# Binding gathered expert rows to their place on two engines in a hybrid decoder layer

## The chip, the cores and the metric

The kernel runs on one core of a Trainium2 chip. Its time is the device time of one launch in microseconds (us), and lower is better. Five engines work side by side, each through a queue of its own that runs in order: TensorE (PE, with its weight loads as PEld), VectorE (DVE), ScalarE (ACT), GpSimd (POOL) and SyncE (SP). SP and POOL also issue DMA transfers. The order within a queue is fixed when the kernel is built.

## The reference, cut to what matters

One decoder layer on 512 tokens of width 1024: an mLSTM and a sliding-window attention share a projection, a cross-attention over 256 memory tokens follows, and then a retrieval from 16,384 experts of one neuron each. All that matters here is the retrieval:

```python
v1, i1 = lax.top_k(s1, 16)            # per token and head: best 16 of 128 first keys
v2, i2 = lax.top_k(s2, 16)            # and of 128 second keys
top_s, pos = lax.top_k(cand_s, 16)    # best 16 of the 256 sums -> expert i1 * 128 + i2
g = jax.nn.softmax(top_s, axis=-1)
u = expert_down[eidx]
a = jax.nn.gelu(jnp.einsum('thkd,td->thk', u, xb), approximate=False)
coef = g * a
return jnp.einsum('thk,thkd->td', coef, expert_up[eidx])
```

There are eight heads, so each token uses 128 experts.

## The kernel before, in words

The 512 tokens are four blocks of 128. The front of the layer, the cross-attention and the top-k run first. The retrieval is then done in two ways.

**Block 0: by rows.** `gather` (line 696) is a generator. Each of its 256 steps fetches one row per token, 128 rows of 4 KB, with an indirect DMA on POOL's queue (`fetch`, line 705), and uses it on DVE: the first 128 steps multiply a row of `expert_down` with the tokens and sum it to one number (`dots`, line 711), and the last 128 add a row of `expert_up`, times its coefficient, to the sum `gacc` (line 721; the first one is line 719). Eight buffers hold rows, so eight fetches can be ahead of DVE.

**Blocks 1 to 3: densely.** For each of the 128 values of the second key, called i2, a "down" tile computes all activations of 128 experts for 384 tokens, and an "up" tile multiplies them with the gates and with the 128 rows of `expert_up`. `Down` (line 755) splits the weights into a high part on ACT (`dh`) and a low part on DVE (`dl`, line 766), runs 24 matmuls, three for each of eight slices of the width (lines 777 to 779), and a Gelu. `up_tile` (line 798) splits its weights in the same way (`uh` on ACT, `ul` on DVE, line 822), multiplies activations by gates on DVE (`cf`, line 829), rounds on ACT (`ch`, line 831) and takes the rest on DVE (`cl`, line 832). `up_mm` (line 836) runs its 18 matmuls. 68 of the 128 down tiles are made early, between other work, and parked in DRAM; five more follow in a lead, and the other 55 are made between the up steps. `up_order` and `made_by(u)` say which tiles go when: `made_by(u)` is the number of down tiles that have been traced by up step u. A ring of ten buffers lets down tiles run ahead of their up steps.

**The gates.** The dense way needs a 128 x 128 table of gates for each token. For block 1, `scatter` (line 611) builds it in DRAM: 128 indirect DMAs on POOL's queue, 16 for each head, add one gate for each token (line 630), and the additions of one head wait for those of the head before. The last 16 are kept in `c.sc[HD - 1]`. For blocks 2 and 3, `gating` (line 639) builds it with one-hots: 32 steps of four tokens for each block, 64 in all. Each step makes a first one-hot for all four tokens (`onehot`, on ACT in even steps and on DVE in odd ones, line 661), four second one-hots times the gate on DVE (line 683, four buffers), and a matmul for each token (line 684). `early.fill(3)` puts nine matmuls of an early down tile behind each step's matmuls.

**What sets the order.** A planner orders each queue on a simulated timeline before the kernel runs. It takes what is ready, earlier code first. `tc.issue_after(x)` restricts it: every instruction that the block under it issues on the engine of x must stand behind x in that queue. It is an order, not a wait. In the kernel before, eight of the 256 row steps are called in the gating of block 3, one in every fourth step (`GEV = 4`), under `issue_after(mm)`. `mm` is a matmul on PE, and a row step issues nothing on PE, so this binds none of its instructions: the planner may put the fetch and the product wherever they seem to fit. The other 248 row steps are called in the first 122 up steps (`GST`), about two for each, behind `c.dl`, the low part of the latest down tile, on DVE. Their fetches on POOL are free.

Of the kernel before, what the change touches and what calls it, by code (L numbers as in the profile page):

```python
# [17 lines left out]
ALU = mybir.AluOpType  # L18
# [3 lines left out]
P = 128  # L22
# [3 lines left out]
NB = S // P  # L26
# [4 lines left out]
HD = 8  # L31
TK = 16
NK = 128
# [10 lines left out]
FGT0 = KT  # L44
# [3 lines left out]
assert SP == SG * UG and (sum(FRT) + FEND) % KT == 0  # L48


GEV = 4
GST = 122

LEAD = 5
# [11 lines left out]
def f32(ap):  # L66
    return ap.bitcast(F32)
# [571 lines left out]
def gating(c, early, ga):  # L639

    nc, ps, gs, mp = c.nc, c.ps, c.gs, c.mp
    V, A, T = nc.vector, nc.scalar, nc.tensor
    for b in range(NG + NS, NB):
        tr = []
        for n_, src in (("I1T", c.I1), ("I2T", c.I2), ("gT", c.gg)):
            tp = ps.tile([P, 512], F32, tag="a", name="tp_i")
            T.transpose(tp[:, :P], src[:, b].rearrange("p h k -> p (h k)"), c.ident)
            o = gs.tile([P, P], F32, tag=n_, bufs=1, name=n_)
            A.copy(o, tp[:, :P])
            tr.append(o)  # L650
        i1, i2, g = tr
        n1 = gs.tile([P, P], F32, tag="n1", bufs=1, name="n1")
        A.mul(n1, i1, -1.0)
        io = c.iota.unsqueeze(1).to_broadcast([P, 4, P])

        def onehot(q):

            o1 = gs.tile([P, 4, P], F32, tag="oh1", bufs=5, name="oh1")
            ib = i1[:, 4 * q:4 * q + 4].unsqueeze(2).to_broadcast([P, 4, P])
            if q % 2:  # L660
                V.tensor_tensor(o1, io, ib, op=ALU.is_equal)
            else:
                for t1 in range(4):
                    t = 4 * q + t1
                    A.activation(o1[:, t1], c.iota, AF.Abs, bias=n1[:, t:t + 1])
                A.activation(o1, o1, AF.Relu, bias=1.0, scale=-1.0)
            return o1

        oh = [onehot(q) for q in range(3)]
        if b == NG + NS:  # L670
            early.fill(FGT0)
        for q in range(32):
            if q % 8 == 0:
                stg = gs.tile([P, NK, 32], F32, tag="stg", bufs=2, name="stg")
            if q + 3 < 32:
                oh.append(onehot(q + 3))
            o1 = oh[q]
            w = ps.tile([P, 512], F32, tag="b", name="w")
            w4 = w.rearrange("p (i t) -> p i t", t=4)
            for t1 in range(4):  # L680
                t = 4 * q + t1
                o2 = gs.tile([P, P], F32, tag="oh2", bufs=4, name="oh2")
                V.tensor_scalar(o2, c.iota, i2[:, t:t + 1], g[:, t:t + 1], op0=ALU.is_equal, op1=ALU.mult)
                mm = T.matmul(w4[:, :, t1], o1[:, t1], o2, start=True, stop=True)
            q8 = q % 8
            A.copy(stg[:, :, 4 * q8:4 * q8 + 4], w4)
            if q8 == 7:
                nc.sync.dma_start(c.wd[b - NG][:, :, 32 * UG * (q // 8):32 * UG * (q // 8 + 1)].rearrange("g p i -> p g i"),
                                  stg.rearrange("p (g i) t -> p g (i t)", i=UG))
            with c.tc.issue_after(mm.ins):  # L690
                early.fill(FGT)
                if b == NB - 1 and q % GEV == GEV - 1:
                    step(ga, 1)


# [29 lines left out]
def split3(c, pool, raw, tag, bufs):  # L725
    hi = pool.tile([P, D], F32R, tag=tag + "h", bufs=bufs, name=tag + "h")
    lo = pool.tile([P, D], F32R, tag=tag + "l", bufs=bufs, name=tag + "l")
    c.nc.scalar.copy(hi, raw)  # L728
    return hi, lo
# [68 lines left out]
def up_tile(c, u, i2, gel, acc):  # L798
    nc, up = c.nc, c.up
    V, A, T = nc.vector, nc.scalar, nc.tensor  # L800
    if i2 % UG == 0:
        c.wt = up.tile([P, ND, UG * P], F32, tag="wt", bufs=2, name="wt")
        for b in range(ND):
            i = nc.sync.dma_start(c.wt[:, b], c.wd[b][i2 // UG])
            for j in c.sc[HD - 1] if b == 0 else ():
                c.tc.add_manual_dep(i.ins, j.ins.name, SYNC, reason="gates complete")
        if i2 < SP:
            c.gsr = c.gl.tile([P, UG, TD], F32, tag="gsr", bufs=2, name="gsr")
            nc.sync.dma_start(c.gsr, c.gd[i2 // UG])
    if i2 % GRP == 0:  # L810
        c.uraw = up.tile([P, GRP, D], F32, tag="uraw", bufs=2, name="uraw")
        nc.sync.dma_start(c.uraw, c.a["up"].rearrange("(i p) d -> p i d", p=P)[:, i2:i2 + GRP])
    g = c.gsr[:, i2 % UG] if i2 < SP else gel[i2]
    raw = c.uraw[:, i2 % GRP]
    last = u == NK - 1
    if last:
        z = c.xlo.rearrange("p k t -> p (k t)")
        hi, lo = z[:, 0:D], z[:, D:2 * D]
        A.copy(hi, raw)
    else:  # L820
        hi, lo = split3(c, up, raw, "u", 2)
    V.tensor_tensor(lo, raw, f32(hi), op=ALU.subtract)  # L822
    cf = up.tile([P, TD], F32, tag="cf", bufs=2, name="cf")
    if last:
        ch, cl = z[:, 2 * D:2 * D + TD], z[:, 3 * D:3 * D + TD]
    else:
        ch = up.tile([P, TD], F32R, tag="ch", bufs=2, name="ch")
        cl = up.tile([P, TD], F32R, tag="cl", bufs=2, name="cl")
    V.tensor_tensor(cf.rearrange("p (b t) -> p b t", t=32), g.rearrange("p (b t) -> p b t", t=32),  # L829
                    c.wt.rearrange("p b (q i t) -> p (b q) i t", q=4, i=UG)[:, :, i2 % UG], op=ALU.mult)  # L830
    A.copy(ch, cf)  # L831
    V.tensor_tensor(cl, cf, f32(ch), op=ALU.subtract)  # L832
    return hi, lo, ch, cl


# [200 lines left out]
def body(tc, a, out, dbg=None):  # L1036
    c = Ctx()
    c.tc, c.nc, c.a = tc, tc.nc, a
    nc = c.nc
    with ExitStack() as st:  # L1040
# [47 lines left out]
        def ahead(n):  # L1088
            for _ in range(n):
                gel.append(Down(c, len(gel)).mm().out())  # L1090

        with ExitStack() as tk:
            c.tk = tk.enter_context(pool("topk"))
            early = Early(c, gel)
# [3 lines left out]
        with pool("gather", side="right") as c.gp:  # L1098
            ga = gather(c)
# [1 line left out]
                gating(c, early, ga)  # L1101
            c.up = st.enter_context(pool("up"))
            assert len(gel) == SP
            ahead(LEAD)
            pst_ = [c.ps.tile([P, 512], F32, tag=t, name="acc_u") for t in "bbbbaa"]
            acc = [[pst_[2 * b], pst_[2 * b + 1]] for b in range(ND)]
            last = []
            g0 = 32 // GEV
            for u, i2 in enumerate(up_order()):
                ahead(made_by(u) - len(gel))  # L1110
                with tc.issue_after(c.dl.ins):
                    step(ga, (2 * P - g0) * (u + 1) // GST - (2 * P - g0) * u // GST)
                parts = up_tile(c, u, i2, gel, acc)
                if u >= NK - 2:
                    last.append(parts)
                else:
                    for b in range(ND):
                        up_mm(c, u, parts, acc, b)
# [15 lines left out]
def made_by(u):  # L1134

    return min(NK, SP + LEAD + (u + 1) * (NK - SP) // NK)
# [16 lines left out]
def step(it, n):  # L1153
    for _ in range(n):
        next(it, None)
# [49 lines left out]
```

## Time and profile before

| | |
|---|---|
| median of 3 runs | 1722.9 us (1717.44 to 1725.04) |
| the profiled execution | 1724.66 us, of which its span 1723.0 us |
| busy: PE, PEld | 1640.4 us (95%), 1428.0 us (83%) |
| busy: DVE, ACT, POOL | 1236.0 us (72%), 724.5 us (42%), 602.9 us (35%) |
| moved by DMA | 400.58 MB, 232 GB/s over the span |
| mean granted TensorE clock | 0.98 |

The span is the time from the first to the last instruction of one execution. Busy shares are means over stages. The front, cross-attention and top-k take up to about 707 us, the gating runs from 713 to 912 us, the lead to 935 us and the up steps to 1704 us. A row of the timeline or of the groups names line, engine, operation, and what it writes and reads; in brackets or behind the bar stands how long the engine was idle before it and what ended that.

### The profile page before, as it was taken

What the parts mean: (1) busy time and instruction counts of PE and PEld (TensorE: products, weight loads), DVE (VectorE), ACT (ScalarE), POOL (GpSimd) and SP (SyncE); (2) the same over time, 40 slices, a digit from 0 to 9 for tenths busy, and PEclk for the clock granted to TensorE, in tenths of its full rate; (3) what the DMA queues carried; (4) which work ended last, traced back from release to release, by engine and by line L of the source; (5) the groups of instructions that cost most, each with busy time, mean ns of one, the idle gap of its engine ahead of it and who ended that gap; (6) DMA issues with size and microseconds to landing.
All of it is one profiled execution on the core that took longest, in us unless ns stands there. A gap on an engine that the chain in (4) does not pass through costs nothing. (4 is left out here: it accounts for less than half of the span.)

```text
span 1723.0 us, 22949 instructions
## 1 busy us (share of the span) xinstructions
PE 1640.4 (95%) x8366; PEld 1428.0 (83%) x8368; DVE 1236.0 (72%) x2701; ACT 724.5 (42%) x1206; POOL 602.9 (35%) x427
## 2 busy tenths in 40 slices
PE   7999999999999999559999999999999999999897
PEld 5776588878999999559998888988888888888676
DVE  5535565464778888557775988878888888888965
ACT  5434544343544544437873333333333333332333
POOL 2000000000027878887003544444444443444400
PEclk9997999999999999879999999999999999999999
DMA  6135035232254435648778999988999998988952
GB/s 208 72 145 220 25 122 174 96 137 111 92 180 120 111 93 135 184 120 264 251 227 299 409 359 350 341 324 341 338 364 375 349 350 336 348 327 315 402 198 86
DMA packets 149105, 400.58 MB, mean 232 GB/s; under 512 B 28144, under 2 KB 62080, under 8 KB 136320
## 3 DMA queue, kind: packets, MB, share of 16 engines
q1 hardware_dynamic: 89232, 255.76, 40.8%
q0 software_dynamic: 55360, 134.32, 23.1%
q10 hardware_dynamic: 4400, 9.04, 1.4%
q8 instruction: 65, 1.06, 0.2%
q14 instruction: 48, 0.39, 0.1%
HBM read 356.28 MB, written 42.80 MB: 232 GB/s over the span
## 5 line engine op out<-in xcount | busy, mean ns | idle before, releaser
L777 PE MATMUL acc_d<-xhi,dh 128*128 128x384 f32 x1024 | 351.2, 343 | 3.6 <-ACT gel L788 3.6
L779 PE MATMUL acc_d<-xhi,dl 128*128 128x384 f32 x1024 | 345.2, 337 | 1.7 <-DVE dl L766 1.7
L778 PE MATMUL acc_d<-xlo,dh 128*128 128x384 f32 x1024 | 344.3, 336 | 0.0
L844 PE MATMUL acc_u<-ul,ch 128*128 128x512 f32 x762 | 295.8, 390 | 5.9 <-DVE ul L822 5.9
L845 PE MATMUL acc_u<-uh,cl 128*128 128x512 f32 x762 | 294.6, 390 | 0.0
L705 POOL DMA_INDIRECT rows<-in_down_r_dram,eidx x128 | 177.7, 1388 | 296.5 <-DVE dots L711 276.4
L630 POOL DMA_INDIRECT wd<-gg,ei x128 | 230.4, 1800 | 138.1 <-DVE ei L624 87.3
L705 POOL DMA_INDIRECT rows<-in_up_dram,eidx x128 | 170.5, 1332 | 189.7 <-DVE gacc L721 167.9
L831 ACT CAST ch<-cf 128x384 fp32r<-128x384 f32 x127 | 65.1, 514 | 382.9 <-PE acc_u L844 230.0
L843 PE MATMUL acc_u<-uh,ch 128*128 128x512 f32 x762 | 216.0, 392 | 9.9 <-ACT uh L728 8.7
L766 DVE TENSOR_TENSOR dl<-draw,dh 128x1024 fp32r<-128x1024 f32 x128 | 156.2, 1222 | 72.5 <-ACT dh L728 60.4
L777 PEld LDWEIGHTS acc_d<-xhi,dh 128*128 128x128 f32 x1024 | 194.0, 189 | 8.9 <-ACT gel L788 4.7
L779 PEld LDWEIGHTS acc_d<-xhi,dl 128*128 128x128 f32 x1024 | 193.3, 189 | 4.7 <-DVE dl L766 2.6
L778 PEld LDWEIGHTS acc_d<-xlo,dh 128*128 128x128 f32 x1024 | 193.8, 189 | 2.6
L728 ACT CAST dh<-draw 128x1024 fp32r<-128x1024 f32 x128 | 134.1, 1049 | 140.6 <-PE acc_d L778 116.1
L711 DVE CUSTOM_DVE_ANT_0 rows<-rows,xn 128x1024 f32<-128x1024 f32 x128 | 153.4, 1219 | 35.1 <-DMA rows<-in_down_r_dram,eidx 35.0
L843 PEld LDWEIGHTS acc_u<-uh,ch 128*128 128x128 f32 x762 | 141.9, 188 | 39.5 <-ACT uh L728 11.2
L844 PEld LDWEIGHTS acc_u<-ul,ch 128*128 128x128 f32 x762 | 142.9, 188 | 37.0 <-DVE ul L822 7.8
L845 PEld LDWEIGHTS acc_u<-uh,cl 128*128 128x128 f32 x762 | 143.1, 188 | 29.1
L721 DVE SCALAR_TENSOR_TENSOR gacc<-rows,coef,gacc 128x1024 f32<-128x1024 f32 x127 | 162.5, 1280 | 0.9
L822 DVE TENSOR_TENSOR ul<-uraw,uh 128x1024 fp32r<-128x1024 f32 x127 | 154.2, 1220 | 7.8 <-ACT uh L728 7.1
L832 DVE TENSOR_TENSOR cl<-cf,ch 128x384 fp32r<-128x384 f32 x127 | 70.8, 558 | 111.3 <-ACT ch L831 107.9
(333 smaller groups left out, 2672.0 us busy)
## 6 DMA issues: line engine op xcount, KB each, us to landing
draw<-in_down_t_dram SPq DMA_DIRECT2D x64, 1024.0 KB
uraw<-in_up_dram SPq DMA_DIRECT2D x64, 1024.0 KB
wt<-wd SPq DMA_DIRECT2D x96, 256.0 KB
wd<-stg SPq DMA_DIRECT2D x8, 2048.0 KB
gd<-gsp SPq DMA_DIRECT2D x17, 768.0 KB
gsr<-gd SPq DMA_DIRECT2D x17, 768.0 KB
wd<-zero ACTq DMA_DIRECT2D x1, 8192.0 KB
raw<-in_w_pq_dram SPq DMA_DIRECT2D x8, 1024.0 KB
```

Source lines behind the costliest of these rows:

```text
L630: i = G.indirect_dma_start(out=out, out_offset=bass.IndirectOffsetOnAxis(ap=ei[:, h, k:k + 1], axis=0), in_=c.gg[:, NG, hh, k:k + 1], in_o ...
L705: G.indirect_dma_start(out=r, out_offset=None, in_=src, in_offset=bass.IndirectOffsetOnAxis(ap=c.eidx[:, j:j + 1], axis=0))
L711: V.tensor_tensor_reduce(r, r, c.xn0, 1.0, 0.0, op0=ALU.mult, op1=ALU.add, accum_out=dots[:, j:j + 1])
L721: V.scalar_tensor_tensor(c.gacc, r, coef[:, j:j + 1], c.gacc, op0=ALU.mult, op1=ALU.add)
L766: c.dl = nc.vector.tensor_tensor(self.lo, raw, f32(self.hi), op=ALU.subtract)
L777: T.matmul(acc[:, :TD], self.hi[:, ks], c.xhi[:, k, NG * P:], start=(k == 0), stop=False)
L778: T.matmul(acc[:, :TD], self.hi[:, ks], c.xlo[:, k, NG * P:], start=False, stop=False)
L779: T.matmul(acc[:, :TD], self.lo[:, ks], c.xhi[:, k, NG * P:], start=False, stop=(k == KT - 1))
L822: V.tensor_tensor(lo, raw, f32(hi), op=ALU.subtract)
L843: T.matmul(acc[b][n], ch[:, t], hi[:, d], start=st, stop=False)
L844: T.matmul(acc[b][n], ch[:, t], lo[:, d], start=False, stop=False)
L845: T.matmul(acc[b][n], cl[:, t], hi[:, d], start=False, stop=sp)
```

## The change

It touches three places, and the counts that go with them.

1. In the gating of block 3, a row step is called in every second step from 9 to 31, twelve in all. Its fetch must stand behind the last addition of `scatter` on POOL, and its product behind the step's last one-hot on DVE. Nothing else moves a row step into the gating.
2. In the lead, eight row steps are spread over the five down tiles, each behind that tile's `c.dl` on DVE.
3. In the up steps, the first row step of step u is bound behind `c.cf`, the product with the gates, and any other behind `c.cl`. The 236 row steps left are spread by `due`, which counts one for each up step and one for each down tile made, up to step 121.

Besides, the 24 matmuls of `early.fill(FGT0)` are bound behind the third transpose of block 2's routes on PE.

```diff
-GEV = 4
+GQ = range(9, 32, 2)
+GLD = 8
 GST = 122
...
-            T.transpose(tp[:, :P], src[:, b].rearrange("p h k -> p (h k)"), c.ident)
+            tr_ = T.transpose(tp[:, :P], src[:, b].rearrange("p h k -> p (h k)"), c.ident)
...
         if b == NG + NS:
-            early.fill(FGT0)
+            with c.tc.issue_after(tr_.ins):
+                early.fill(FGT0)
...
-                V.tensor_scalar(o2, c.iota, i2[:, t:t + 1], g[:, t:t + 1], op0=ALU.is_equal, op1=ALU.mult)
+                last = V.tensor_scalar(o2, c.iota, i2[:, t:t + 1], g[:, t:t + 1], op0=ALU.is_equal, op1=ALU.mult)
...
             with c.tc.issue_after(mm.ins):
                 early.fill(FGT)
-                if b == NB - 1 and q % GEV == GEV - 1:
+            if b == NB - 1 and q in GQ:
+                with c.tc.issue_after(c.sc[HD - 1][-1].ins), c.tc.issue_after(last.ins):
                     step(ga, 1)
...
-    V.tensor_tensor(cf.rearrange("p (b t) -> p b t", t=32), g.rearrange("p (b t) -> p b t", t=32),
+    c.cf = V.tensor_tensor(cf.rearrange("p (b t) -> p b t", t=32), g.rearrange("p (b t) -> p b t", t=32),
...
-    V.tensor_tensor(cl, cf, f32(ch), op=ALU.subtract)
+    c.cl = V.tensor_tensor(cl, cf, f32(ch), op=ALU.subtract)
...
-            ahead(LEAD)
+            for n in range(LEAD):
+                ahead(1)
+                with tc.issue_after(c.dl.ins):
+                    step(ga, GLD * (n + 1) // LEAD - GLD * n // LEAD)
...
-            g0 = 32 // GEV
+            g0 = len(GQ) + GLD
+
+            due = [u + made_by(u) for u in range(-1, GST)]
+            rows = [(2 * P - g0) * (d - due[0]) // (due[-1] - due[0]) for d in due]
+            rows += [rows[-1]] * (NK - GST)
             for u, i2 in enumerate(up_order()):
                 ahead(made_by(u) - len(gel))
-                with tc.issue_after(c.dl.ins):
-                    step(ga, (2 * P - g0) * (u + 1) // GST - (2 * P - g0) * u // GST)
                 parts = up_tile(c, u, i2, gel, acc)
+                for i in range(rows[u + 1] - rows[u]):
+                    with tc.issue_after((c.cf if i == 0 else c.cl).ins):
+                        step(ga, 1)
```

## The prediction

> **What bounds the kernel now.** I read the page's 40 slices first, for the place where TensorE does not work.
>
> ```profile
> PE   7999999999999999559999999999999999999897
> ...
> PEclk9997999999999999879999999999999999999999
> ```
>
> PE is full in nearly every slice of 43 us. Two stand out, the 17th and 18th (689 to 775 us): PE at half, and a lower granted clock. They lie where the gating begins, and the change works there. The windows view, cut at the first matmul of the gating and at the point from which its steps run evenly, shows the size. Columns: stretch, length, busy time of each engine with its count, granted clock, DMA share, GB/s.
>
> ```profile
> core 0: us, PE busy (x) PEld busy (x) DVE busy (x) ACT busy (x) POOL busy (x), PEclk, DMA share, GB/s
> 713.35:777.83 64.48, 33.06 (x170) 31.24 (x171) 26.68 (x64) 19.76 (x43) 53.81 (x36) 0.71 0.52 127
> 777.83:905.50 127.67, 127.67 (x886) 127.67 (x886) 93.68 (x252) 98.53 (x215) 28.36 (x18) 1.00 0.79 244
> 911.70:934.70 23.00, 20.97 (x116) 19.58 (x114) 10.53 (x15) 10.69 (x16) 3.67 (x2) 1.00 0.93 332
> 934.00:1260.00 326.00, 324.27 (x1590) 288.65 (x1591) 268.52 (x396) 112.89 (x156) 154.73 (x110) 1.00 0.93 354
> 1260.00:1580.00 320.00, 312.80 (x1507) 273.86 (x1506) 273.14 (x298) 110.61 (x150) 148.69 (x112) 1.00 0.92 349
> 1580.00:1640.00 60.00, 49.95 (x215) 39.42 (x214) 55.77 (x62) 18.91 (x27) 22.70 (x17) 1.00 0.94 367
> 1640.00:1704.00 64.00, 64.00 (x284) 53.01 (x283) 37.86 (x52) 24.45 (x36) 0.57 (x1) 1.00 0.43 149
> ```
>
> From 777.83 us on PE is full: 127.67 us for 886 matmuls, 0.144 us each, so a gating step of 17 (8 for the gates, 9 of the early fill) takes 2.45 us. In the stretch before, 170 matmuls of the same mix took 64.48 us. The up steps are bound by PE too, up to 1580 us; from there to 1640 us DVE is busy for 55.77 of 60 us and PE is not. So PE sets the time, and what can be won is its idle time.
>
> Who stops PE in the first stretch is in DVE's timeline (start, length, instruction, idle before it and what ended that):
>
> ```profile
> 710.43 1.11 DVE L683 TENSOR_SCALAR oh<-iota,I2T,gT 128x128 f32<-128x128 f32 x4
> 726.74 1.23 DVE L711 CUSTOM_DVE_ANT_0 rows<-rows,xn 128x1024 f32<-128x1024 f32 x1 [15.20 <-DMA rows<-in_down_r_dram,eidx]
> ...
> 742.04 1.12 DVE L683 TENSOR_SCALAR oh<-iota,I2T,gT 128x128 f32<-128x128 f32 x4 [0.74 <-PE w L684]
> 762.13 1.23 DVE L711 CUSTOM_DVE_ANT_0 rows<-rows,xn 128x1024 f32<-128x1024 f32 x1 [18.98 <-DMA rows<-in_down_r_dram,eidx]
> ```
>
> Twice DVE stands for 15 and 19 us at the product of a gathered row. The one-hots behind it, which PE needs, stand too. POOL's timeline says why the rows are late:
>
> ```profile
> 722.28 1.04 POOL L705 DMA_INDIRECT rows<-in_down_r_dram,eidx  x1 [0.30 <-issue]
> ...
> 726.13 1.61 POOL L630 DMA_INDIRECT wd<-gg,ei  x1 [0.30 <-issue]
> ...
> 757.81 1.00 POOL L705 DMA_INDIRECT rows<-in_down_r_dram,eidx  x1 [0.30 <-issue]
> ...
> 769.78 2.28 POOL L630 DMA_INDIRECT wd<-gg,ei  x1 [0.30 <-issue]
> ...
> 801.33 2.17 POOL L630 DMA_INDIRECT wd<-gg,ei  x1 [0.30 <-issue]
> ```
>
> The fetches stand between the gate additions of `scatter`. The planner put the products early in DVE's queue and the fetches between additions that it thought quicker than they are.
>
> **The change, part by part.**
>
> *1. The wait in the gating goes.* In the new kernel a row step in the gating begins at step 9 of block 3, the 42nd of 64, and no row step of the lead or the up steps can be earlier on DVE, since their products stand behind a low part of the lead or behind `cf` and `cl`. So no product stands before the first 41 steps, and these 170 matmuls should take 170 x 0.144 = 24.5 us. That is 64.48 - 24.5 = **40.0 us** less. The next thing that could be late there is the fetch for step 9. Without the three fetches from 722.28 and the eight from 757.81 (3.85 and 11.97 us), the last addition ends at 801.33 + 2.17 - 15.8 = 788 us. A fetch took 4.5 us from issue to use (722.28 to 726.74), so a row is there at 792 us; the one-hots of step 9 come at about 713 + 41 x 2.45 = 813 us. That leaves 20 us. If the steps did not return to full pace, the gain would be PE's idle time alone:
>
> ```profile
> PE w L684 <- DVE oh L683: 31.4, 6, 17.1
> ```
>
> ```profile
> 713.36 2.08 PE L684 MATMUL w<-oh,oh 128*128 128x128 f32 x8 [3.70 <-ACT oh L666]
> ...
> 777.84 1.05 PE L684 MATMUL w<-oh,oh 128*128 128x128 f32 x8
> ```
>
> These 31.4 us are what PE waited for one-hots, and 40.0 - 31.4 = 8.6 us is slower work: the granted clock was 0.71 in the stretch, and the first eight matmuls behind a wait took 2.08 us against 1.05 later. The Trainium skill, in TensorE: Matmul & The Clock Gate, section "Part 1: The HAM clock gate", says that the clock halves after an idle window of about 3.4 us and comes back after as long a time of work; the 3.70 us before the first gate matmuls and DVE's two long waits would then cost about 1.7 us each by its figures, an estimate of 5.1 us, and this term would be 36.5 us. The trace shows more than that rule, and I take the trace: 40.0, with 31.4 as the other end.
>
> *2. The 24 matmuls behind the transposes.*
>
> ```profile
> 705.12 0.35 DVE L586 TENSOR_TENSOR I<-eq 128x64 f32<-128x64 bf16 x2
> ```
>
> ```profile
> 706.99 0.38 PE L647 MATMUL tp_i<-ident,I 128*128 128x128 f32 x2
> ```
>
> The transposes could start when the routes are written, at 705.5 us, and start at 706.99. Moved behind them, the 24 matmuls (3.5 us at 0.144 each) fall into the 3.70 us that PE waits for the first one-hot. At best that is -1.5 us; if they run at the low clock they reach past the one-hot, at worst +2. I take **-1**.
>
> *3. Twelve rows in 23 gating steps.* A product took 1.23 us, so twelve are some 15 us of DVE in 23 x 2.45 = 56 us. DVE was busy for 93.68 of 127.67 us, 73%, so 15 us are free. It just fits, on an engine that also waits for PE's buffers. I take **+1**; with no cover at all it is +15.
>
> *4. Eight rows in the lead.* DVE was busy for 10.53 of 23.00 us, so eight rows, 10 us, fit into the 12.5 that are free. But DMA is at 0.93, and gates and weights for the first up step are loaded then. I take **+1**, from -2.0 (all of PE's idle time) to +5 (half of the rows uncovered).
>
> *5. The up steps to 1580 us.* The groups of DVE from 934 to 1580 us (busy, mean ns, idle before):
>
> ```profile
> L711 DVE CUSTOM_DVE_ANT_0 rows<-rows,xn 128x1024 f32<-128x1024 f32 x116 | 138.9, 1219 | 0.0
> L721 DVE SCALAR_TENSOR_TENSOR gacc<-rows,coef,gacc 128x1024 f32<-128x1024 f32 x102 | 130.5, 1280 | 0.8
> ...
> L832 DVE TENSOR_TENSOR cl<-cf,ch 128x384 fp32r<-128x384 f32 x100 | 55.7, 558 | 85.6 <-ACT ch L831 83.1 <-PE acc_u L845 2.1 <-issue 0.2
> ```
>
> 100 up steps stood here, with 218 rows. PE's idle time in the two rows of the windows is 1.7 + 7.2 = 8.9 us. In the new spread the 100th step (u = 99, 119 down tiles) is at 99 + 119 - 72 = 146 of 177 units, so 195 of the 236 rows are behind it: 23 fewer, 29 us less for DVE in 646. I take **-4** of the 8.9; the ends are -8.9 and, should a row in front of `cl` now and then hold PE up, +10.
>
> *6. The last row steps.*
>
> ```profile
> L721 DVE SCALAR_TENSOR_TENSOR gacc<-rows,coef,gacc 128x1024 f32<-128x1024 f32 x25 | 32.0, 1279 | 0.1
> L822 DVE TENSOR_TENSOR ul<-uraw,uh 128x1024 fp32r<-128x1024 f32 x11 | 13.4, 1218 | 0.0
> L832 DVE TENSOR_TENSOR cl<-cf,ch 128x384 fp32r<-128x384 f32 x12 | 6.7, 556 | 5.3 <-ACT ch L831 4.5 <-PE acc_u L845 0.7
> L829 DVE TENSOR_TENSOR cf<-gsr,wt 128x384 f32<-128x384 f32 x8 | 4.4, 554 | 0.1
> ```
>
> ```profile
> L766 DVE TENSOR_TENSOR dl<-draw,dh x128: 1202/1220/1298, 381.0 to 1553.9; 128x1024 fp32r<-128x1024 f32 x128
> ```
>
> These are DVE's groups from 1580 to 1640 us, and the tile view of `dl`. The last down tile was split at 1553.9 us: the planner had run them ahead of their place in the code, which goes to step 117. After that an up step is 18 matmuls of 64.00 / 284 = 0.225 us, 4.06 us of PE. In the 60 us stand 215 matmuls, 11.9 steps, so a step took 5.02 us, on DVE: 1.22 + 0.55 + 0.56 + 2.09 rows of 1.28 us = 5.0. PE lost 60 - 215 x 0.225 = 11.6 us. The new spread counts down tiles where the code has them, not where they run. From the 101st to the 122nd step it leaves 236 - 195 = 41 rows, 1.86 a step. If down tiles run ahead as before, a step takes 5.02 - 0.23 x 1.28 = 4.73 us, 0.67 over PE's, in 22 steps 14.8 us: **+3.2** against the 11.6. If they don't, a step has 1.33 rows and 4.05 us, which PE covers: -11.6. The other end is +8, for steps a quarter us slower still.
>
> **The sum**, against the profiled execution's 1724.66 us: -40.0 - 1 + 1 + 1 - 4 + 3.2 = -39.8, so 1684.9. The median of the three runs, 1722.9, lies 1.8 below that execution, so I expect **1683 us**.
>
> **The rivals.**
>
> A, the forecast: the stall goes, the rest nearly balances. 1683 us, own range 1671 to 1696.
>
> B, the up steps gain as well: the new places hold the down tiles to their code order, or fill DVE's waits for `ch` so well that PE never waits. Terms 5 and 6 are then -8.9 and -11.6: 1663 us. For it speaks that DVE idles 83.1 us in front of `cl`, just where a row bound behind `cf` would go; against it, that nothing binds the down tiles on PE.
>
> C, the twelve rows are not covered. DVE becomes the bound in the last 23 gating steps, and term 3 is +15: 1697 us. For it speaks that 15 us meet 15 us of free time on an engine that also waits for buffers; against it, that the one-hots may be a whole step ahead of PE.
>
> D, slower: a row bound in front of `cl` makes each up step late. `cl` waited 0.83 us for `ch` on average (83.1 in 100 steps); a row of 1.28 us there hides that and adds 0.45 us, and in 122 steps, if all of it reaches PE, 55 us: 1738 us. It decides from 39.8 / 122 = 0.33 us a step on. Against it: the buffers let `cl` be a step ahead of PE, 4.06 us, and before, rows stood in front of `cl` as well.
>
> E, the stall moves to step 9: the additions end later than I think, and its row holds DVE again. From 769.78 to 801.33 us an addition took 2.10 us, with DVE at work, 16 in this stretch; the 32 that were left at 722.28 us, at that rate, end by 790 us. At 2.7 us each the margin is gone, and at 3.15 the wait is 15 us: 1698 us. The Trainium skill, in SBUF - State Buffer, section "Who interferes with whom", speaks for this: GpSimd and VectorE share a pair of ports, and some VectorE instructions block GpSimd for their whole length, so additions should be slower beside steadily working one-hots. Between the two fetch groups, where DVE mostly stood, 16 additions took 31.7 us, 1.98 each, so the trace bears this out by 0.12 us only.
>
> F, the change does not do what it says: the edges of two nested blocks don't both hold and the products stay early. 1723 us. Nothing speaks for it but that the old block bound nothing either.
>
> **How the numbers follow.** A 0.66, B 0.14, C 0.10, D 0.05, E 0.03, F 0.02. A measurement of this kernel can tell about 0.5%, 8.6 us, from no change. A, B, C and E are faster by more: 0.93. F is the same, 0.02, and D slower, 0.05. The range from 1663 to 1704 us takes in B, A and C with the unknown ends of terms 3 to 6, and leaves out D, F and the outer edges.
>
> **What would show it.** Term 1: no idle time in front of L711 put down to DMA, all 128 additions without a fetch between them, the last done near 790 us, a granted clock of 1.00 and the 64 gating steps done by about 870 us instead of 912. Term 3: PE idle by no more than 2 us in the last 23 gating steps. Terms 5 and 6: the last row near step 122, PE idle about 5 us up to the last `dl` and about 15 us behind it; with B almost none. The prediction is wrong if DVE still waits for a row in the gating, or if PE's idle time in front of L843 to L845 grows by over 20 us.

## The result, and the profile after

The changed kernel took **1677.36 us** (median of 4 runs, 1676.78 to 1678.69) beside 1723.97 us (1717.44 to 1727.39) for the kernel before: a ratio of 0.9735, 95% interval 0.9705 to 0.9765. The forecast was 1683, with 1663 to 1704 around it. The profiled execution after took 1678.69 us, of which its span is 1676.9, so 46.1 us less span than before.

The page's slices again, here of 42 us each. The two half-empty slices of PE are gone, and so is the dip of the granted clock beside them.

```profile
PE   7999999999999999999999999999999999999987
...
PEclk9997999999999999999999999999999999999999
```

The windows view, cut at the same events as before: the first gate matmul, the end of the gating, then the up steps.

```profile
core 0: us, PE busy (x) PEld busy (x) DVE busy (x) ACT busy (x) POOL busy (x), PEclk, DMA share, GB/s
712.15:872.07 159.92, 159.92 (x1105) 159.69 (x1104) 128.21 (x332) 119.39 (x260) 92.70 (x59) 1.00 0.86 267
872.07:903.15 31.08, 25.97 (x132) 24.50 (x131) 20.60 (x32) 10.97 (x16) 13.27 (x10) 0.89 1.01 369
905.00:1240.00 335.00, 335.00 (x1632) 296.70 (x1632) 264.24 (x392) 118.59 (x163) 136.03 (x102) 1.00 0.91 344
1240.00:1560.00 320.00, 320.00 (x1541) 281.14 (x1540) 258.93 (x283) 111.48 (x154) 133.23 (x100) 1.00 0.89 331
1560.00:1600.00 40.00, 39.07 (x170) 31.43 (x169) 40.00 (x47) 12.36 (x17) 28.21 (x19) 1.00 1.01 393
1600.00:1640.00 40.00, 34.99 (x145) 27.55 (x144) 34.66 (x42) 14.00 (x21) 8.08 (x7) 0.96 0.84 325
```

PE is busy in every one of the 159.92 us of the gating, at full clock. It has no idle time in the up steps until 1560 us, and 0.93 + 5.01 us from there to 1640. But the stretch between gating and up steps, the lead, is 31.08 us, where it was 23.00, and has 5.1 us of idle time.

What PE waited for from 700 to 905 us (engine and line, released by, total, times, longest):

```profile
PE acc_d L780 <- ACT dh L731: 3.6, 1, 3.6
PE tp_i L648 <- DVE iu L621: 2.6, 1, 2.6
PE acc_d L780 <- ACT gsp L795: 1.0, 1, 1.0
```

The 31.4 us for one-hots have left no trace in it. The rows of DVE and POOL that answer to those of before (start, length, instruction, idle time before it):

```profile
810.86 1.29 DVE L685 TENSOR_SCALAR oh<-iota,I2T,gT 128x128 f32<-128x128 f32 x4 [1.02 <-PE w L686]
811.89 1.22 DVE L714 CUSTOM_DVE_ANT_0 rows<-rows,xn 128x1024 f32<-128x1024 f32 x1
```

```profile
724.01 1.54 POOL L631 DMA_INDIRECT wd<-gg,ei  x1 [2.29 <-DVE oh L685]
...
756.42 1.54 POOL L631 DMA_INDIRECT wd<-gg,ei  x1 [0.30 <-issue]
766.18 1.59 POOL L631 DMA_INDIRECT wd<-gg,ei  x1 [8.22 <-issue]
...
799.58 2.16 POOL L631 DMA_INDIRECT wd<-gg,ei  x1 [0.30 <-issue]
802.05 1.62 POOL L708 DMA_INDIRECT rows<-in_down_r_dram,eidx  x1 [0.30 <-ACT oh L667]
```

The first product stands behind the one-hots of its step without any idle time in front of it. All 128 additions come first and the first fetch behind them; but the last addition ends at 801.74 us, not near 788, because POOL stands still for 8.22 us at the first addition of the last head, and for 2.29 us at that of the head before. The 32 additions of these two heads are slower as well: from the first to the last of a head they take 34.0 and 35.6 us, where it was 31.4 and 33.7.

To compare kernels I use three spans between starts of matmuls, which don't depend on when an execution reached the gating: **gating** (first to last gate matmul, `w`), **lead** (to the first `uh,ch` matmul of `acc_u`), **up** (to the last of these). The rows of the tile view they come from, before and then after:

```profile
L684 PE MATMUL w<-oh,oh x512: 272/275/582, 713.4 to 911.4; 128*128 128x128 f32 x171
L843 PE MATMUL acc_u<-uh,ch x762: 387/389/499, 934.7 to 1704.4; 128*128 128x512 f32 x191
```

```profile
L686 PE MATMUL w<-oh,oh x512: 270/275/356, 712.2 to 871.8; 128*128 128x128 f32 x171
L846 PE MATMUL acc_u<-uh,ch x762: 387/389/610, 903.2 to 1658.3; 128*128 128x512 f32 x191
```

| kernel | median us (runs from, to) | ratio to before, 95% interval | gating | lead | up |
|---|---|---|---|---|---|
| before | 1723.97 (1717.44, 1727.39) | | 198.0 | 23.3 | 769.7 |
| after | 1677.36 (1676.78, 1678.69) | 0.9735 [0.9705, 0.9765] | 159.6 | 31.4 | 755.1 |
| gating rows alone | 1683.64 (1681.8, 1684.87) | 0.976 [0.9739, 0.9781] | 160.4 | 24.6 | 766.8 |
| up steps alone | 1718.62 (1713.65, 1720.52) | 0.9958 [0.9944, 0.9972] | 197.9 | 22.6 | 767.0 |
| product bound only | 1676.94 (1675.2, 1679.12) | 0.972 [0.97, 0.9741] | 160.0 | 31.2 | 755.4 |
| fetch bound only | 1733.24 (1728.1, 1737.22) | 1.0053 [1.004, 1.0067] | 216.2 | 29.2 | 755.5 |
| rows nine steps earlier | 1690.37 (1683.58, 1691.82) | 0.98 [0.9783, 0.9816] | 174.9 | 29.2 | 754.7 |
| additions ahead of transposes | 1679.57 (1676.48, 1681.08) | 0.9729 [0.971, 0.9747] | 161.8 | 31.9 | 753.5 |
| spread by where tiles run | 1680.84 (1675.66, 1682.39) | 0.9732 [0.9713, 0.9751] | 160.0 | 31.3 | 759.3 |
| even spread | 1676.17 (1674.31, 1680.25) | 0.9717 [0.9698, 0.9735] | 160.2 | 31.3 | 754.3 |
| old place in the step | 1687.69 (1687.51, 1689.68) | 0.9784 [0.9768, 0.9801] | 159.9 | 31.6 | 764.5 |
| no rows in lead | 1676.73 (1673.01, 1678.59) | 0.9711 [0.9693, 0.973] | 159.2 | 25.0 | 761.7 |
| sixteen rows in gating | 1671.55 (1671.01, 1672.76) | 0.9687 [0.9674, 0.9701] | 159.6 | 23.7 | 757.0 |
| a row in each gating step | 1672.89 (1670.74, 1676.7) | 0.9705 [0.9689, 0.9721] | 167.6 | 22.0 | 752.0 |

Each ratio is to runs of the kernel before in the same round (their medians go from 1723.97 to 1725.57 us).

From before to after: -1.2 to the first gate matmul, -38.4 in the gating, +8.1 in the lead, -14.6 in the up steps, together -46.1, the whole difference of the spans. The gain is in the gating, as forecast, but the lead and the up steps together gave another 6.5 us, which the forecast did not have.

### The profile page after: what moved, and what is told of

Its sections match the earlier page's. It is cut to its first block, busy times and chain, and to the rows that moved or that the text cites. A ratio compares the mean times of both kernels' runs of the same rounds, so it can differ in the third digit from the quotient of the medians.

```text
span 1676.9 us, 22996 instructions
## 1 busy us (share of the span) xinstructions
PE 1638.2 (98%) x8368; PEld 1427.2 (85%) x8368; DVE 1227.4 (73%) x2701; ACT 722.5 (43%) x1206; POOL 601.7 (36%) x427
## 3 DMA queue, kind: packets, MB, share of 16 engines
q8 instruction: 65, 1.06, 0.3%
## 4 chain that ended last, share of the span: by engine, by line
PE 92%; DVE 3%; DMA 2%; issue 2%; ACT 1%; SPq 0%; DVEq 0%; POOLq 0%; POOL 0%; ACTq 0%
PE acc_d L782 10%; PE acc_d L780 10%; PE acc_d L781 10%; PE acc_u L847 9%; PE acc_u L846 9%; PE acc_u L848 9%; PE acc_f L946 4%; PE acc_f L948 4%; PE acc_f L947 4%; PE w L686 3%; PE acc_t L959 2%; PE acc_t L961 2%; PE acc_t L960 2%; PE sp L300 1%; PE o_att L334 1%
## 5 line engine op out<-in xcount | busy, mean ns | idle before, releaser
L847 PE MATMUL acc_u<-ul,ch 128*128 128x512 f32 x762 | 299.2, 393 | 2.3 <-DVE ul L825 2.3
L848 PE MATMUL acc_u<-uh,cl 128*128 128x512 f32 x762 | 298.4, 392 | 0.0
L631 POOL DMA_INDIRECT wd<-gg,ei x128 | 234.4, 1831 | 148.4 <-DVE ei L625 87.3
L708 POOL DMA_INDIRECT rows<-in_down_r_dram,eidx x128 | 167.5, 1309 | 253.2 <-DVE dots L714 235.9
L708 POOL DMA_INDIRECT rows<-in_up_dram,eidx x128 | 175.5, 1371 | 214.3 <-DVE gacc L724 189.5
```

Source lines behind the costliest of these rows:

```text
L631: i = G.indirect_dma_start(out=out, out_offset=bass.IndirectOffsetOnAxis(ap=ei[:, h, k:k + 1], axis=0), in_=c.gg[:, NG, hh, k:k + 1], in_o ...
L708: G.indirect_dma_start(out=r, out_offset=None, in_=src, in_offset=bass.IndirectOffsetOnAxis(ap=c.eidx[:, j:j + 1], axis=0))
L847: T.matmul(acc[b][n], ch[:, t], lo[:, d], start=False, stop=False)
L848: T.matmul(acc[b][n], cl[:, t], hi[:, d], start=False, stop=sp)
```

## Experiments

My theory after the result: in the gating DVE's queue decides, since it takes its instructions in order and a product whose row is missing holds the one-hots behind it; in the up steps the new place behind `cf` lets a row fill the time in which DVE waits for ScalarE's copy. Rivals: in the gating it was the fetches among POOL's additions; in the up steps it was the twelve rows taken out, or the new spread. Each diff below shows "-" for the changed kernel and "+" for the experiment, unless it says otherwise. The two parts came first.

**Gating rows alone.** The kernel before, with only the gating's part of the change.

```diff
# against the kernel before
...
-                if b == NB - 1 and q % GEV == GEV - 1:
+            if b == NB - 1 and q in GQ:
+                with c.tc.issue_after(c.sc[HD - 1][-1].ins), c.tc.issue_after(last.ins):
                     step(ga, 1)
...
```

> The kernel before with the first part of the change alone: twelve rows in the gating, bound behind the last addition on POOL and the step's one-hots on DVE; the lead and the up steps as before, with 244 rows spread evenly behind dl. Theory (the gain is the wait of DVE for rows in the gating, some 38 us, and the up steps bring the rest): 64 gating steps in about 160 us instead of 198, PE idle in the up steps still 15 to 18 us, and 1685 us. Rival (the up steps bring most of it): over 1700 us.

It took 1683.64 us. The gating is 160.4, and the lead (24.6) and the up steps (766.8) are close to those of before.

**Up steps alone.** The kernel before, with the new places and the new spread in the up steps, 248 rows as before.

```diff
# against the kernel before
+            due = [u + made_by(u) for u in range(-1, GST)]
...
-                with tc.issue_after(c.dl.ins):
-                    step(ga, (2 * P - g0) * (u + 1) // GST - (2 * P - g0) * u // GST)
                 parts = up_tile(c, u, i2, gel, acc)
+                for i in range(rows[u + 1] - rows[u]):
+                    with tc.issue_after((c.cf if i == 0 else c.cl).ins):
+                        step(ga, 1)
```

> The new kernel with its gating, its lead and its early matmuls put back as before (eight free rows in the gating); the up steps new, with 248 rows. Theory: DVE waits 35 us for rows in the gating as before, PE's idle time in the up steps falls from 18 to about 6 us, and 1711 us. Rival (the up steps bring most): under 1700 us. If the two parts help each other, the gains of this run and of the gating alone do not add up to the 46.6 us of the whole.

It took 1718.62 us, so 7.6 us of the gain that I gave to this part are not there: the up steps went from 769.7 to 767.0 only. The two ratios, 0.024 and 0.0042 below one, add up to 0.028, beside 0.0265 for the whole change. So nine tenths of the result are the gating rows.

**Product bound only, fetch bound only.** The two edges of the gating's rows, one at a time.

```diff
# product bound only
-                with c.tc.issue_after(c.sc[HD - 1][-1].ins), c.tc.issue_after(last.ins):
+                with c.tc.issue_after(last.ins):
# fetch bound only
-                with c.tc.issue_after(c.sc[HD - 1][-1].ins), c.tc.issue_after(last.ins):
+                with c.tc.issue_after(c.sc[HD - 1][-1].ins):
```

> The new kernel, with the gating's rows bound on DVE alone; in the planned order of POOL three fetches then stand behind the 96th addition and five behind the 112th. Theory (only the place of the product counts, not that of the fetch): no wait of DVE for a row, the last addition about 10 us later than in the new kernel, no change in time, 1677 us. Rival (fetches among the additions cost by themselves): 5 us or more above it.

> The new kernel, with the gating's rows bound on POOL alone; in the planned order of DVE the first product then stands behind the 16th gating step and the twelfth behind the 23rd. Theory: the first product waits until the last addition and one fetch are through (about 795 us, with additions at 1.85 us while DVE stands), while step 16 is over at about 751 us: a wait of about 45 us on DVE and PE, longer than in the kernel before, and 1723 to 1730 us. Rival (it was the fetches among the additions): 1677 us, as in the new kernel.

With the product bound and the fetches left among the additions, the time is 1676.94 us, the same. The last addition was then issued at 796.48 us, 3.1 earlier than in the changed kernel, not 10 later as I had written: fetches among the additions cost them nothing here. With the fetch bound and the product free, the kernel is slower than before by half a percent, 1733.24 us (ratio 1.0053, 1.004 to 1.0067). Waits of DVE and of PE in that kernel, 700 to 940 us:

```profile
DVE rows L714 <- DMA rows<-in_down_r_dram,eidx: 48.4, 2, 48.1
...
PE w L686 <- DVE oh L685: 51.1, 6, 48.0
```

The planner put the first product at step 16, and it stood there for 48.1 us until the row came. This pair settles the gating: what costs the time is the place of the consumer in DVE's queue. Binding the producer alone makes it worse, because the row now comes only behind the last addition, while its product still stands at step 16.

**Rows nine steps earlier.** If that is so, the price of a place that is too early can be worked out.

```diff
-GQ = range(9, 32, 2)
+GQ = range(0, 23, 2)
```

> The changed kernel with its twelve rows of the gating bound behind the one-hots of the last block's steps 1, 3, ... 23 instead of 10, 12, ... 32; the first place comes at about 790 us, before the last addition lands. Theory (a row's place only has to be later than the landing of its fetch, and VectorE waits for what is missing): the additions end at 795 to 802 us as in the runs so far, the first row lands 4.4 us after its fetch was issued, so VectorE stands at the first product for 9 to 16 us and PE for nearly as long; the time is 1677 plus that and up to 4 us for matmuls at a lower clock, 1686 to 1697 us. Rival (what cost the time was the order of the fetches among the additions, not VectorE standing at a product): the wait is hidden by the buffers between VectorE and PE, and the time is 1677 us, within 3.

```profile
PE w L686 <- DVE oh L685: 13.0, 1, 13.0
...
DVE rows L714 <- DMA rows<-in_down_r_dram,eidx: 14.7, 1, 14.7
```

It took 1690.37 us, 13.0 more than the changed kernel. The gating is 15.3 us longer (174.9), 13.0 of them PE's wait and 2.3 work at a lower clock. The profiled execution, at 1683.58 us the shortest of the four, had reached the gating 7.6 us earlier (first transpose at 697.80 us instead of 705.38), so only its spans are compared; the other three runs took 1690.10 to 1691.82. In this execution the first fetch was issued at 792.4 us and the product began at 797.1, 4.7 us later. Put on the clock of the changed kernel, whose first fetch is at 802.05, a row is there at 806.7 and is used at 811.9: the change has a margin of about **5 us, two gating steps**, not 20.

**Additions ahead of transposes.** The smallest edge of the change undone.

```diff
-            with c.tc.issue_after(tr_.ins):
-                early.fill(FGT0)
+            early.fill(FGT0)
```

> The changed kernel without the binding of the 24 down matmuls behind the three transposes of the gating, which are then where the kernel before has them. Theory (the binding gains what PE would have waited for the first one-hot): the gating begins at 713.4 us instead of 712.2 and the rest is the same; the time is 1.2 us longer, less than these rounds can tell, so the trace decides. Rival (the 24 matmuls that stand behind the transposes run at a lower clock and take back what was won): the gating begins at the same time, within 0.3 us.

The rows of PE, first of this kernel and then of the changed one:

```profile
712.85 2.07 PE L685 MATMUL w<-oh,oh 128*128 128x128 f32 x8 [3.70 <-ACT oh L667]
```

```profile
705.38 0.41 PE L648 MATMUL tp_i<-ident,I 128*128 128x128 f32 x2 [2.62 <-DVE iu L621]
...
712.16 1.06 PE L686 MATMUL w<-oh,oh 128*128 128x128 f32 x8
```

The gating began 0.7 us later and was 2.2 us longer, since its first matmuls then run at the low clock (2.07 us for eight instead of 1.06). Counted from the start of `iu` (line 621 of the changed kernel), for which the transposes wait, to the last gate matmul, it is 169.7 us (704.88 to 874.6) against 166.7 (705.15 to 871.8) with the edge; the kernel with the gating rows alone, which lacks the edge too, has 168.4 (704.28 to 872.7). So by these traces the edge is worth 2 to 3 us; the ratios of the whole time, 0.9729 and 0.9735, cannot tell. The theory's sign holds, its 1.2 us were too small, and the rival falls: the 24 moved matmuls do run slowly (0.32 us apart until 709.61 us, 0.174 from there), but they take that upon themselves instead of the gate matmuls.

**Four runs on the up steps and the lead.**

```diff
# spread by where tiles run
-            due = [u + made_by(u) for u in range(-1, GST)]
+AHD = 8
...
+            due = [u + min(NK, made_by(u) + AHD) for u in range(-1, GST)]
# no rows in lead
-GLD = 8
+GLD = 0
# even spread
-            due = [u + made_by(u) for u in range(-1, GST)]
+            due = list(range(GST + 1))
# old place in the step
-                    with tc.issue_after((c.cf if i == 0 else c.cl).ins):
+                    with tc.issue_after(c.dl.ins):
```

> The changed kernel with the rows of the up steps spread evenly over 122 steps, as in the kernel before; the places behind the products of gates stay. By count this moves next to nothing: 193 instead of 195 of 236 rows stand behind the 100th step. Theory (the place in the step is what fills PE's idle time up to 1560 us, not the spread): 1677 us, within 2, with PE idle for 0 to 2 us up to 1560 us. Rival (the spread by down tiles does it, putting rows where down tiles cover them): 1682 us or more, with 4 to 9 us of idle time of PE up to 1580 us as before.

> The changed kernel with its spread, but the rows of an up step bound behind the last split of a down tile again, as in the kernel before, and not behind the two products of gates. Theory (the place in the step does it: before, VectorE stood 83.1 us in 100 steps waiting for ScalarE's copy, and a row in that place costs only the rest): PE is idle for 5 to 9 us up to 1560 us again, and the time is 1682 to 1686 us. Rival (what filled PE's idle time is that twelve more rows were taken out of the up steps): PE stays without idle time up to 1560 us, and the time is 1677 us, within 2.

The even spread changes nothing (1676.17 us). The old place costs 10.3 us (1687.69), more than I had expected. Only the edge is the old one here: a row step is still called behind `up_tile`, while the kernel before called it ahead of it, and whether that adds to the cost was not tried. The place is also worth less in other kernels of the table: by their up steps 2.7 us with 248 rows (before, up steps alone) and 5.1 with 244 (gating rows alone, no rows in lead), beside 9.4 here with 236. These are its up steps, and its groups of DVE from 905 to 1560 us (count, busy, mean ns, idle before); the same groups of the changed kernel follow.

```profile
905.00:1240.00 335.00, 330.78 (x1616) 292.85 (x1614) 270.62 (x397) 118.00 (x161) 144.00 (x109) 1.00 0.93 351
1240.00:1560.00 320.00, 313.06 (x1509) 274.47 (x1507) 275.41 (x290) 110.78 (x152) 142.22 (x113) 1.00 0.92 347
```

```profile
L724 DVE SCALAR_TENSOR_TENSOR gacc<-rows,coef,gacc 128x1024 f32<-128x1024 f32 x115 | 147.2, 1280 | 0.9
L714 DVE CUSTOM_DVE_ANT_0 rows<-rows,xn 128x1024 f32<-128x1024 f32 x104 | 124.7, 1219 | 0.0
...
L835 DVE TENSOR_TENSOR cl<-cf,ch 128x384 fp32r<-128x384 f32 x102 | 56.8, 557 | 74.2 <-ACT ch L834 71.7 <-PE acc_u L848 1.0 <-PE acc_d L782 0.6
```

```profile
L714 DVE CUSTOM_DVE_ANT_0 rows<-rows,xn 128x1024 f32<-128x1024 f32 x105 | 127.0, 1221 | 0.0
...
L724 DVE SCALAR_TENSOR_TENSOR gacc<-rows,coef,gacc 128x1024 f32<-128x1024 f32 x97 | 124.2, 1280 | 0.4
...
L835 DVE TENSOR_TENSOR cl<-cf,ch 128x384 fp32r<-128x384 f32 x104 | 57.9, 557 | 107.8 <-ACT ch L834 107.7
```

So the place matters, as I had said, and for another reason than I had said. If rows filled DVE's wait for `ch`, that wait would have become shorter; it is longer, 107.7 us against 71.7. What differs is the count: in the same 655 us, with the same spread in the code, the old place had 115 + 104 = 219 rows done and the new one 97 + 105 = 202. The tile view gives the last row of each, old place first:

```profile
L724 DVE SCALAR_TENSOR_TENSOR gacc<-rows,coef,gacc x127: 1272/1280/1324, 1233.1 to 1587.3; 128x1024 f32<-128x1024 f32 x127
```

```profile
L724 DVE SCALAR_TENSOR_TENSOR gacc<-rows,coef,gacc x127: 1272/1280/1302, 1254.6 to 1633.4; 128x1024 f32<-128x1024 f32 x127
```

The planner runs down tiles ahead of their place in the code, and a row bound behind `dl` runs ahead with them: 46 us ahead at the end. There DVE has more to do early, when it must feed down and up tiles at once (PE idle for 4.2 + 6.9 us), and little at the end. Bound behind `cf` and `cl`, rows keep the pace of the up steps. The rows that run ahead are shown; that they are what makes PE wait is what fits best, as the next run bears out. The waits of ACT from 905 to 1560 us fit it too, here of the old place and then of the changed kernel:

```profile
ACT gel L791 <- DVE cf L832: 60.4, 31, 3.0
```

```profile
ACT gel L791 <- DVE cf L832: 15.7, 11, 2.8
```

The Gelu of a down tile waits for a buffer of the ring, which `cf` on DVE frees, and the splits `uh` stand behind it in ACT's queue. PE's waits of the old place in this stretch are 7.4 us for `uh`, 2.0 for `ul` on DVE and 1.6 for `gel`; none is put down to a transfer.

> The changed kernel, with its rows in the up steps spread by where the down tiles really run, eight ahead of their place in the code: 204 instead of 195 of the 236 rows stand behind the 100th up step, so 32 instead of 41 are left for the last 22. Theory (in the last steps, where no down tiles are left on PE, VectorE sets the pace, and earlier it has free time): PE's idle time from 1560 to 1640 us, 9.45 us now, goes to 2 to 4 us, and up to 1560 us it stays near 0, so the time is about 1671 us. Rival (VectorE has as little to spare before as after, 9 rows of 1.28 us each are only moved): what is won at the end comes back as idle time of PE before 1560 us, and the time stays at 1677 us, within 2.

```profile
1240.00:1560.00 320.00, 314.48 (x1512) 275.35 (x1512) 259.58 (x279) 109.83 (x151) 146.71 (x103) 1.00 0.89 333
1560.00:1600.00 40.00, 34.99 (x151) 27.67 (x150) 33.92 (x40) 12.38 (x17) 17.73 (x13) 1.00 0.89 336
1600.00:1640.00 40.00, 39.11 (x172) 32.03 (x172) 34.70 (x41) 13.20 (x18) 5.85 (x4) 1.00 0.82 294
```

The rival was right. The nine rows moved ahead cost PE 5.5 us before 1560 us, and at the end 5.9 us of idle time are left, as many as in the changed kernel. The up steps are 4.2 us longer; the median is 3.5 us longer, beyond the rival's 2, though the ratio (0.9732) is that of the changed kernel.

> The changed kernel without the eight rows between the gating and the first up step; the 244 rows that are left are spread over the up steps. Theory (these rows cost the stretch its time: their transfers delay the one that PE waits for through ScalarE, 6.15 us in the changed kernel): the stretch from the end of the gating to the first up matmul goes from 31.1 us back to about 23 us with PE idle for some 2 us, while the up steps have eight more rows, 10 us of VectorE, of which at most 5 us reach PE; 1672 to 1679 us. Rival (the stretch is longer because 16 more matmuls were put into it, and its wait has another cause): PE is still idle for about 5 us there, and the time is 1677 to 1682 us.

Without rows in it the lead is 6.4 us shorter (25.0), and PE's wait for `dh` there is 1.5 us instead of 3.6. But the up steps are 6.6 us longer with the eight rows, and the time is the same, 1676.73 us. So a row costs as much in the lead as in the up steps, 0.8 us by these spans, in which 12 matmuls of down tiles moved along (120 instead of 132 in the lead). The theory holds for the place of the loss, but its 5 us at most for the up steps were too few, and nothing is won.

**More rows in the gating.** If a row costs as much in either place, it should go where it costs nothing.

```diff
-GQ = range(9, 32, 2)
-GLD = 8
+GQ = [q for q in range(9, 32) if q % 3 != 2]   # sixteen; or range(9, 32), a row in each
+GLD = 0
...
-            due = [u + made_by(u) for u in range(-1, GST)]
+            due = list(range(GST + 1))
```

> The changed kernel with sixteen rows in the last 23 steps of the gating (two in three steps) instead of twelve, none between gating and up steps, and 240 spread evenly over 122 up steps. Theory (VectorE's busy time is what decides in the gating): it is busy for 60.26 of the 69 us behind 803 us, four rows more make 65.2 us, which still fits, so the gating is at most 2 us longer; the stretch to the first up matmul is 24 instead of 31 us, the up steps have four rows more, 5 us; the time is 1673 to 1678 us. Rival (waits for buffers eat the free time, so that PE stands for each row more): the gating is 4 to 5 us longer, and the time is 1679 us or more.

> The changed kernel with a row in each of the last 23 steps of the gating, none between gating and up steps, and 233 spread evenly over 122 up steps. Theory (VectorE's busy time decides): eleven rows more make 60.26 + 13.5 = 73.7 us of work in 69 us, so VectorE sets the pace and the gating is 5 to 9 us longer, with PE waiting for one-hots; 7 us are won back before the first up matmul only in part, since 3 of them were idle time; the time is 1679 to 1684 us. Rival (the one-hots run so far ahead that PE does not feel it): the gating is at most 2 us longer, and with three rows less in the up steps the time is 1670 to 1675 us.

The windows of the kernel with sixteen rows; then that of the one with a row in each step, with what its PE waited for from 700 to 910 us:

```profile
803.00:872.00 69.00, 68.15 (x468) 67.72 (x467) 63.69 (x157) 47.39 (x101) 23.71 (x22) 1.00 1.03 372
872.10:895.50 23.40, 20.82 (x117) 19.76 (x116) 9.20 (x12) 10.47 (x15) 1.81 (x2) 1.00 0.99 350
```

```profile
803.00:872.00 69.00, 63.93 (x421) 61.39 (x420) 67.97 (x162) 45.40 (x96) 28.03 (x25) 1.00 1.05 387
```

```profile
PE w L686 <- DVE oh L685: 5.1, 7, 0.9
```

Sixteen rows fit: DVE is busy for 63.69 of 69 us, and the gating is 159.6 us long, the same. The lead is 7.7 us shorter and the up steps 1.9 longer, together -5.8, and 1677.36 - 1671.55 is 5.8, for four rows fewer in lead and up steps. **This kernel is the fastest**: 1671.55 us, 0.9687 [0.9674, 0.9701] of the kernel before. It and the changed kernel were timed against before in different rounds, and their intervals just don't touch. With a row in every step DVE is full, 67.97 of 69 us, PE waits 5.1 us for one-hots in 7 places, and the gating is 8.0 us longer. Here the theory was right on the gating and wrong on the time (1672.89 us, where it had 1679 to 1684): it had given the lead and the up steps too little, which are 9.4 and 3.1 us shorter, together 12.5 for eleven rows fewer. So taken out of both places a row gives 1.1 to 1.5 us.

## Why the prediction was right, point by point

- **Term 1, the stall, -40.0:** right, -38.4 (-37.6 with the gating rows alone, without the edge of term 2). Of these 31.4 is PE's waiting, as quoted, and 7.0 the slower work, which I had put at 8.6; it is half of the 13.9 us that PE worked at the low clock (last section).
- **Term 2, the 24 matmuls, -1:** right in sign, too small. The gating begins 1.2 us earlier, and from `iu` to its end the edge is worth 2 to 3 us.
- **Term 3, twelve rows in the gating, +1:** right. PE is never idle from 803 us to the end of the gating, and with sixteen rows the gating is as long as with twelve. What rival C feared came only with 23 rows, and as 8.0 us.
- **Term 4, eight rows in the lead, +1:** mis-sized. The lead is 8.1 us longer, beyond the end of +5. By 872.07:903.15, 16 more matmuls stand in it than before (132 instead of 116; at 0.174 us each, 2.8 us, which the up steps then lack), 3.1 us more idle time, and a clock of 0.89, which makes the other 2.2. I had compared free time of DVE with the rows' length; but `dh` came late and `dl` with it, in a stretch in which DMA is at 1.01.
- **Terms 5 and 6, the up steps, -4 and +3.2:** mis-sized. PE has no idle time up to 1560 us, the better end of term 5 (-8.9), and 5.9 us behind it, against 10.05 from 1580 to 1640 us before, so -4.1 where term 6 had +3.2. Over all the up steps PE's idle time went from 18.3 to 6.0 us; the other 2.3 of the -14.6 are 21 matmuls fewer, most of them moved into the lead. The failed step is that I priced the places by DVE's load and the spread, and said of the down tiles only that they run ahead. That rows bound behind `dl` run ahead with them, and that the new places end this, I had not seen. In term 6 the price of a step was right: from 1560 us to the end of the last row, 1634.7 us, 290 matmuls make 16 steps of 4.6 us, where I had 4.73. But such steps were 16, not 22, and in them PE was idle for 5.9 us, not 14.8; why so few is open. The even spread shows that the new spread itself is worth nothing. Not all of the -14.6 is the place, either: with the old place and as many matmuls moved into the lead, 236 rows instead of 248 took the up steps from 769.7 to 764.5.
- **The sum:** -39.8 forecast, -46.1 measured. The gating and what leads to it were -40.0 forecast with terms 1 to 3 and are -39.6; the lead and the up steps were +0.2 and are -6.5. That is the whole difference, and it lies inside the range of the likeliest case, 1671 to 1696 us.
- **The margin, 20 us:** wrong, about 5. I took the whole length of the removed fetches (15.8 us) off the end of the additions, as if POOL's queue had been full. Where they had stood, POOL now waits, 8.22 us at the first addition of the last head and 2.29 at that of the head before, and the additions of these heads take 4.4 us more. The last addition ends 1.8 us earlier than before, and with the margin of 5 us nothing came of it.
- **The rivals:** D falls, since PE's idle time went down with rows in front of `cl`. E did not come, but by the margin a place three steps earlier would have brought it; nine steps earlier, the stall was back with 14.7 us. The slower additions it feared came as 2.1 and 2.2 us each, not 2.7. F falls with the first row of DVE above. Of B only the -8.9 came, and by neither of its ways: the down tiles still run ahead (the last split at 1517.5 us, 141 us ahead of the end of the span `up`, where it was 151 before), and DVE's wait for `ch` from 905 to 1560 us grew from 82.3 to 107.7 us.

## What to carry to other kernels

On an engine that takes its queue in order, bind the instruction that uses the data to a place where the data must have come; binding the transfer alone moved it later and left its user standing (1733 us against 1677). When work is bound behind an instruction that a planner may run ahead, it runs ahead with it, so bind it to the loop whose pace it should keep, and count in the trace what was done by when. Price a movable piece in each stage by trying it there: here a row cost about 1 us in the lead or in the up steps (0.8 to 1.5 by the kernels compared) and nothing in the gating, until DVE was full at between 16 and 23 rows.

## What the runs showed of the hardware

- The granted clock was low for whole multiples of 3.41 us. By windows of 0.2 us, it was 0.50 in the gating of the kernel before in four stretches, of 3.42, 13.65, 17.07 and 3.42 us, which are 1, 4, 5 and 1 times 3.41; their starts are 2, 9 and 7 such steps apart. In the changed kernel it was low from 706.32 to 709.74 us, 3.42 again. No long wait was needed: in the 3.41 us ahead of the last stretch PE worked for 1.89 us and no wait was longer than 0.90 us. The second stretch began 2.3 us after the last matmul had ended (717.51 us). The four stretches, and the 3.41 us ahead of the last:

```profile
712.96:716.38 3.42, 3.02 (x12) 3.02 (x13) 0.00 (x0) 1.98 (x4) 3.07 (x2) 0.50 0.79 223
719.79:733.44 13.65, 3.65 (x13) 3.35 (x14) 5.89 (x14) 1.16 (x4) 11.21 (x9) 0.50 0.47 116
750.51:767.58 17.07, 3.81 (x15) 3.84 (x16) 5.45 (x12) 1.73 (x5) 14.02 (x11) 0.50 0.55 143
774.40:777.82 3.42, 3.42 (x11) 3.42 (x12) 1.33 (x5) 2.39 (x6) 2.81 (x3) 0.50 1.13 344
770.99:774.40 3.41, 1.89 (x11) 1.21 (x9) 3.41 (x8) 0.00 (x0) 3.11 (x2) 1.00 1.07 372
```

  The Trainium skill, in TensorE: Matmul & The Clock Gate, section "Part 1: The HAM clock gate", has about 3.4 us of idle time for the halving and as much work for the return. The return agrees with the trace; the halving came after less.
- The slower work is half of what PE does in these stretches: 3.02 + 3.65 + 3.81 + 3.42 = 13.9 us, half of it 6.9, where 38.4 us less 31.4 us of waits leaves 7.0. With the rows nine steps earlier, PE worked 5.2 us at the low clock (790.15 to 803.81 us), half 2.6, beside 2.3. With the fetch bound it is 5.0 us (754.04 to 805.24 us), half 2.5, beside 5.5, and 3 us stay open. The price doesn't grow in step with the length of the wait.
- POOL's stop in front of the last head's additions, 8.22 us, has no releaser in the profile. It stands where one head's additions must wait for those of the head before; its cause was not tried.
